# A 3x3 convolution on one core: output channels dealt to even and odd partitions, stored by halves

## The chip, the cores and the metric

The kernel runs on one core of a Trainium2 chip. The metric is the device time of the whole program in microseconds (us). The kernel before has a median of 126.94 us over 8 runs, from 126.81 to 127.33 us. The profile comes from one profiled execution with a time of 126.81 us; its trace spans 125.0 us, so 1.81 us of that time lie around the span.

## The reference

```python
batch, c_in, h, w, c_out = 16, 64, 64, 64, 128
x_pad = np.pad(x, ((0, 0), (0, 0), (1, 1), (1, 1)))
for b, co, ci, kh, kw:
    output[b, co] += weight[co, ci, kh, kw] * x_pad[b, ci, kh:kh+h, kw:kw+w]
```

(The five loops are drawn into one line here.) Input and output are float32. The input is 16 images of 64 channels, 64 x 64 pixels (16.8 MB); the output is 16 images of 128 channels, 64 x 64 pixels (33.6 MB). One channel of one image is 16,384 bytes, contiguous in memory, and a whole output image is 2 MB.

## The kernel before

The 16 images are worked on in 8 pairs, p = 0 to 7. The 64 channels of the first image of a pair stand in partitions 0 to 63, those of the second in partitions 64 to 127. The convolution is computed row pair by row pair with sums of two input rows (`sums`, tile `ss`), so that each block of 8 row pairs needs three groups of matmuls (`group`): one over `ss`, one for the even output rows and one for the odd ones. ScalarE copies the first group out of PSUM (tile `ut`, L188). VectorE adds it to the second group (L194) and to the third (L197) and writes the output tile `ot` in SBUF. `ot` has 128 partitions, one for each output channel, and per partition two images of 64 rows of 64 float32 values. Four such blocks make a pair.

**Weights.** The weights arrive as `w_raw`, one output channel per partition. VectorE casts them to float16 (`w16`, L88). Eighteen matmuls at L116 transpose them: the stationary operand is a slice of `w16`, the moving operand the 128 x 128 identity `ident`, which GpSimd makes. The column in which an output channel comes out in `wp` and then in `Wt` is the partition of `ot` in which it is computed; with `ident` channel c is in partition c.

**Input.** `load` (L63) brings a pair as one transfer of 2 MB, the first pair in four cuts. ScalarE casts it to float16 (tile `xs`, L75), and two pieces are cast by GpSimd. The first seven pairs are asked for at the start; the last, LATE = 7, when the store of pair 2 has been issued.

**Output.** When the last block of a pair is done, the pair is stored. All transfers, loads and stores, go through one queue, SyncE's (SP), in program order (`keep`). A store waits in that queue for the VectorE addition before it. Pairs 0 to 4 and 6 go out in one transfer each (L210: 128 partitions, two images of 16 KB each per partition). Pair 7 goes in two, after 32 and after 64 rows. Pair 5 is cut differently: its first image in one transfer (L205), the first 58 rows of its second image in another (L206), and the last 6 rows in two more (L208), of 124 and of 4 partitions. Four slots of 32 KB per partition hold first the input and then the output tiles: `ot` of pair p is in slot (p + 3) % 4.

**Transfers and semaphores.** In the built program the transfers take eight completion semaphores in rotation, and a transfer waits for the one that used its semaphore before it, eight transfers earlier. Loads and stores count alike.

Of the kernel before, what the change touches and what calls it, by code (L numbers as in the profile page):

```python
# [9 lines left out]
F16 = mybir.dt.float16  # L10
# [3 lines left out]
def kernel(  # L14
# [6 lines left out]
    nc = tc.nc  # L21
    B, CI, H, W = x.shape
    CO = weight.shape[0]
# [3 lines left out]

    keep = tc.keep_in_program_order
    x_rows = x.rearrange("b c h w -> (b c) h w")
    out_pairs = out.rearrange("(g b) co h w -> g co b h w", b=2)  # L30
    w_flat = weight.rearrange("co ci kh kw -> co (ci kh kw)")

    const = ctx.enter_context(tc.tile_pool(name="const", bufs=1))
# [20 lines left out]
    def load(p):  # L54
        if p >= 6:
            xf[p] = big.tile([128, H, W], F32, tag="single", name="xf")
        else:
            if p % 2 == 0:
                two[p // 2] = pair_slot(p // 2, [128, 2, H, W], "xf")
            xf[p] = two[p // 2][:, p % 2, :, :]  # L60
        for lo, hi in cuts if p == 0 else [(0, H)]:
            keep(
                nc.sync.dma_start(  # L63
                    xf[p][:, lo:hi, :], x_rows[128 * p : 128 * p + 128, lo:hi, :]
                )
            )
# [3 lines left out]
    def cast(p, n):  # L70
        if p not in xs:
            xs[p] = xpool.tile([128, H, W], F16, tag=f"xs{p % 4}", name="xs")
        lo, hi = cuts[n]
        copy = nc.gpsimd.tensor_copy if (p, n) in by_pool else nc.scalar.copy
        keep(copy(xs[p][:, lo:hi, :], xf[p][:, lo:hi, :]))  # L75
# [3 lines left out]
    def outs(p):  # L79
        ots[p] = pair_slot((p + 3) % 4, [128, 2, H // 2, 2, W], "ot")  # L80
# [3 lines left out]
    outs(0)  # L84
    ident = const.tile([128, 128], F16)
    make_identity(nc, ident)
    w16 = const.tile([CO, CI * 9], F16)
    keep(nc.vector.tensor_copy(w16, w_raw))  # L88

# [3 lines left out]
    def sums(eng, p, src, lo, n):  # L93
        if p not in ss:
            ss[p] = spool.tile([128, H // 2, W], F16, tag="ss", name="ss")
        v = src.rearrange("p (j i) c -> p j i c", i=2)
        keep(
            eng.tensor_add(  # L98
                ss[p][:, lo : lo + n, :], v[:, lo : lo + n, 0, :], v[:, lo : lo + n, 1, :]
            )  # L100
        )
# [9 lines left out]
    for kh in (1, 2, 0):  # L111
        wp = psum.tile([128, 512], F32, tag="acc", name="wp")
        for k in range(3):
            t = 3 * kh + k
            for q in (0, 64):
                nc.tensor.matmul(wp[q : q + 64, k * CO : k * CO + CO], w16[:, t::9], ident)  # L116
        wps[kh] = wp[:, 0 : 3 * CO]
    keep(nc.scalar.copy(wrow(G1), wps[1]))  # L118
    sums(nc.vector, 0, xf[0], 0, RB)
# [16 lines left out]
    for p in range(NP):  # L136
        if p not in ots:
            outs(p)
        if p + 1 < NP:
            for lo in (0, 16):  # L140
                sums(nc.gpsimd, p + 1, xf[p + 1] if p in (0, 1, 6) else xs[p + 1], lo, 16)
            if p == 1 or p == 2:
                cast(2 * p + 1, 3)
        for blk in range(4):
            j0 = blk * RB

            def group(wi_rows):

                tiles = [
                    psum.tile([128, RB, W], F32, tag="acc", name="acc") for _ in range(2)  # L150
                ]
                n = 3 * len(wi_rows)
                i = 0
                for wi, off in wi_rows:
                    for kw in (1, 0, 2):
                        c_lo, c_hi = max(0, 1 - kw), min(W, W + 1 - kw)
                        for b2 in range(2):
                            p0 = 64 * b2
                            lo, hi = j0, j0 + RB
                            if off is None:  # L160
                                rhs = ss[p][p0 : p0 + 64, lo:hi, c_lo + kw - 1 : c_hi + kw - 1]
                            else:
                                while 2 * lo + off < 0:
                                    lo += 1
                                while 2 * (hi - 1) + off > H - 1:
                                    hi -= 1
                                first = 2 * lo + off
                                last = 2 * (hi - 1) + off
                                rhs = xs[p][
                                    p0 : p0 + 64,  # L170
                                    first : last + 1 : 2,
                                    c_lo + kw - 1 : c_hi + kw - 1,
                                ]
                            nc.tensor.matmul(  # L174
                                tiles[b2][:, lo - j0 : hi - j0, c_lo:c_hi],
                                Wt[p0 : p0 + 64, wi, kw, :],
                                rhs,
                                start=i == 0,
                                stop=i == n - 1,
                            )  # L180
                        i += 1
                return tiles

            U = group([(G1, None)])
            us = []
            for b2 in range(2):
                ut = upool.tile([128, RB, W], F32, tag="ut", name="ut")
                keep(nc.scalar.copy(ut, U[b2]))  # L188
                us.append(ut)
            for q, n in casts[p][blk]:  # L190
                cast(q, n)
            A = group([(G21, 1), (G0, -1)])
            for b2 in range(2):
                nc.vector.tensor_add(ots[p][:, b2, j0 : j0 + RB, 0, :], A[b2], us[b2])  # L194
            Bt = group([(G01, 0), (G2, 2)])
            for b2 in range(2):
                nc.vector.tensor_add(ots[p][:, b2, j0 : j0 + RB, 1, :], Bt[b2], us[b2])  # L197
            parts = {3: (0, 64)} if p < NP - 1 else {1: (0, 32), 3: (32, 64)}
            if blk in parts:
                lo, hi = parts[blk]  # L200
                src = ots[p].rearrange("p b j i c -> p b (j i) c")
                dst = out_pairs[p]
                if p == 5:

                    keep(nc.sync.dma_start(dst[:, 0, :, :], src[:, 0, :, :]))  # L205
                    keep(nc.sync.dma_start(dst[:, 1, 0:58, :], src[:, 1, 0:58, :]))  # L206
                    for q0, q1 in ((0, 124), (124, 128)):
                        keep(nc.sync.dma_start(dst[q0:q1, 1, 58:64, :], src[q0:q1, 1, 58:64, :]))  # L208
                else:
                    keep(nc.sync.dma_start(dst[:, :, lo:hi, :], src[:, :, lo:hi, :]))  # L210
                if p == 2:
                    load(LATE)
# [28 lines left out]
```

## Time and profile before

| what | value |
|---|---|
| median of 8 runs, lowest, highest | 126.94, 126.81, 127.33 us |
| profiled execution: own time, span | 126.81, 125.0 us |
| TensorE busy, share of the span | 105.5 us, 84% |
| VectorE busy | 84.2 us, 67% |
| ScalarE busy | 65.5 us, 52% |
| GpSimd busy | 33.4 us, 27% |
| last VectorE addition, start and length of the last two | 110.99 us, 1.28 us |
| issue of the last store | 112.30 us |
| bytes read from and written to HBM | 17.07 MB, 33.55 MB |
| DMA packets | 4338, 50.77 MB |

The profile counts an engine as busy while one of its instructions runs. The DMA engines, 16 for the core, have a row of their own with their mean busy share, and one with the rate. Two views name what the end of the program hangs on: the chain of work that ended last, which is followed back from the last instruction, and the table of stretches, which gives for any stretch of time the busy time of each engine and the busy share of the DMA engines. The records under these views hold each DMA packet with its start, its length and its size, but not the DMA engine that moved it. A packet of 4 bytes is a completion mark: each DMA engine that takes part in a transfer writes one when its part is done.

### The profile page before, as it was taken

To read this page: it belongs to the slowest core of one execution; us is meant where nothing else is said; L and a number is where in the kernel's file an instruction comes from. 1 tells how busy PE (TensorE), PEld (TensorE's weight loads), DVE (VectorE), ACT (ScalarE), POOL (GpSimd) and SP (SyncE) were. 2 spreads that over 40 slices of the span, in tenths; PEclk is the share of its full clock that TensorE was granted. 3 is DMA by queue.
4 is the path that set the end of the run, shared out by engine and by line. 5 is a ranking of instruction groups with operands and counts; after the bars stand their busy time and mean duration, and the time that the engine had idled before them with its cause. 6 is when DMAs were issued, how large, how long until landed. Compare 5 with 4: busy or idle time off the path is not lost.

```text
span 125.0 us, 2428 instructions
## 1 busy us (share of the span) xinstructions
PE 105.5 (84%) x978; PEld 53.3 (43%) x978; DVE 84.2 (67%) x135; ACT 65.5 (52%) x98; POOL 33.4 (27%) x22
## 2 busy tenths in 40 slices
PE   0489999999999999999999999999999999940000
PEld 0334545545555455455554555445454554510000
DVE  0288777777777777777877787778777788870000
ACT  4283899999789886666333333334666533300000
POOL 2000396930870075006700570049000000000000
PEclk9999999999999999999999999999999999999555
DMA  4999999999999999999999999999999999999981
GB/s 115 314 437 440 430 425 419 430 446 425 425 430 422 419 438 435 430 430 419 414 425 446 430 419 440 430 419 419 435 435 421 429 407 432 427 417 419 427 375 50
DMA packets 4338, 50.77 MB, mean 406 GB/s; under 512 B 360, under 2 KB 488, under 8 KB 1128
## 3 DMA queue, kind: packets, MB, share of 16 engines
q1 hardware_dynamic: 4328, 50.63, 96.4%
q8 instruction: 7, 0.11, 0.3%
q14 instruction: 3, 0.02, 0.0%
HBM read 17.07 MB, written 33.55 MB: 405 GB/s over the span
## 4 chain that ended last, share of the span: by engine, by line
PE 82%; DMA 4%; DVE 2%; issue 1%; DVEq 0%; SPq 0%
PE acc L174 82%; DMA xf<-in_x_dram 4%; DVE ot L194 1%; DVE ss L98 1%; DVE ot L197 0%; DVEq L236 0%; SPq L48 0%; DVEq L194 0%
## 5 line engine op out<-in xcount | busy, mean ns | idle before, releaser
L174 PE MATMUL acc<-xs,Wt 64*128 64x504 f16 (+3 forms) x768 | 88.3, 376 | 0.0
L174 PEld LDWEIGHTS <-Wt 64*128 64x128 f16 x960 | 52.2, 95 | 52.9 <-issue 2.8
L194 DVE TENSOR_TENSOR ot<-acc,ut 128x512 f32<-128x512 f32 x64 | 41.2, 686 | 21.6 <-PE acc L174 18.0
L188 ACT COPY ut<-acc 128x512 f32<-128x512 f32 x64 | 34.4, 590 | 39.3 <-issue 35.2
L197 DVE TENSOR_TENSOR ot<-acc,ut 128x512 f32<-128x512 f32 x64 | 41.1, 684 | 0.0
L75 ACT CAST xs<-xf 128x1024 f16<-128x1024 f32 (+2 forms) x30 | 30.9, 1065 | 0.6 <-DMA xf<-in_x_dram 0.6
L174 PE MATMUL acc<-ss,Wt 64*128 64x504 f16 (+1 forms) x192 | 27.0, 384 | 1.1 <-DVE ss L98 1.1
L98 POOL TENSOR_TENSOR ss<-xs 128x1024 f16<-128x1024 f16 x8 | 16.8, 2127 | 30.4 <-PE acc L174 30.4
L98 POOL TENSOR_TENSOR ss<-xf 128x1024 f16<-128x1024 f32 x6 | 14.1, 2369 | 23.2 <-DMA xf<-in_x_dram 14.6
L116 PE MATMUL wp<-ident,w 128*64 128x128 f16 x18 | 1.3, 328 | 4.3 <-DVE w L88 4.3
L98 DVE TENSOR_TENSOR ss<-xf 128x512 f16<-128x512 f32 x4 | 2.8, 689 | 2.6 <-DMA xf<-in_x_dram 2.6
L88 DVE CAST w<-w_raw 128x576 f16<-128x576 f32 x1 | 0.5, 460 | 3.7 <-DMA w_raw<-in_weight_dram 3.7
L116 PEld LDWEIGHTS <-w 128*64 128x64 f16 x18 | 1.1, 210 | 4.3 <-DVE w L88 4.3
L118 ACT CAST Wt<-wp 128x384 f16<-128x384 f32 x1 | 0.5, 480 | 2.9 <-PE wp L116 2.9
L75 POOL CAST xs<-xf 128x896 f16<-128x896 f32 x2 | 1.9, 934 | 0.0
L118 ACT ACT_TABLE_LOAD x1 | 1.3, 1283 | 0.7 <-PEq L225 0.7
L123 ACT CAST Wt<-wp 128x384 f16<-128x384 f32 x1 | 0.5, 479 | 0.5 <-DVE Wt L121 0.5
L120 DVE TENSOR_TENSOR Wt<-wp,Wt 128x384 f16<-128x384 f32 x1 | 0.6, 551 | 0.0
L121 DVE TENSOR_TENSOR Wt<-wp,Wt 128x384 f16<-128x384 f32 x1 | 0.5, 548 | 0.0
L124 ACT CAST Wt<-wp 128x384 f16<-128x384 f32 x1 | 0.5, 484 | 0.0
masks.py:199 POOL TENSOR_SCALAR_AFFINE_SELECT ident<-ident 128x128 f16<-128x128 f16 x1 | 0.3, 292 | 0.1
masks.py:197 POOL MEMSET ident<- 128x128 f16 x1 | 0.2, 204 | 0.3 <-POOLq L225 0.3
(4 smaller groups left out, 0.4 us busy)
## 6 DMA issues: line engine op xcount, KB each, us to landing
out_dram<-ot SPq DMA_DIRECT2D x6, 4096.0 KB, 20.8
xf<-in_x_dram SPq DMA_DIRECT2D x7, 2048.0 KB, 21.0
out_dram<-ot SPq DMA_DIRECT2D x3, 2048.0 KB, 13.5
out_dram<-ot SPq DMA_DIRECT2D x1, 1856.0 KB, 17.7
xf<-in_x_dram SPq DMA_DIRECT2D x2, 512.0 KB, 5.7
xf<-in_x_dram SPq DMA_DIRECT2D x1, 576.0 KB, 4.8
xf<-in_x_dram SPq DMA_DIRECT2D x1, 448.0 KB
w_raw<-in_weight_dram SPq DMA_DIRECT2D x1, 288.0 KB, 3.0
```

Of the source, the lines that this page charges most:

```text
L75: keep(copy(xs[p][:, lo:hi, :], xf[p][:, lo:hi, :]))
L88: keep(nc.vector.tensor_copy(w16, w_raw))
L98: eng.tensor_add(ss[p][:, lo : lo + n, :], v[:, lo : lo + n, 0, :], v[:, lo : lo + n, 1, :])
L116: nc.tensor.matmul(wp[q : q + 64, k * CO : k * CO + CO], w16[:, t::9], ident)
L118: keep(nc.scalar.copy(wrow(G1), wps[1]))
L120: keep(nc.vector.tensor_sub(wrow(G21), wps[2], wrow(G1)))
L121: keep(nc.vector.tensor_sub(wrow(G01), wps[0], wrow(G1)))
L123: keep(nc.scalar.copy(wrow(G0), wps[0]))
L174: nc.tensor.matmul(tiles[b2][:, lo - j0 : hi - j0, c_lo:c_hi], Wt[p0 : p0 + 64, wi, kw, :], rhs, start=i == 0, stop=i == n - 1,)
L188: keep(nc.scalar.copy(ut, U[b2]))
L194: nc.vector.tensor_add(ots[p][:, b2, j0 : j0 + RB, 0, :], A[b2], us[b2])
L197: nc.vector.tensor_add(ots[p][:, b2, j0 : j0 + RB, 1, :], Bt[b2], us[b2])
```

## The change

The weights are transposed with another matrix, `spread`, in place of `ident`. `spread` is a copy of `ident` with its columns reordered, so that output channel e * 64 + q (e = 0 or 1, q = 0 to 63) comes out in partition 2q + e. Channels 0 to 63 are thus in the even partitions of `ot`, channels 64 to 127 in the odd ones. Each store becomes two: e = 0 stores the even partitions, which is 64 channels that lie side by side in memory, and e = 1 the odd ones. Of pair 5, the even half goes out in one transfer; the odd half is cut into its first image, the first 56 rows of its second image, and the last 8 rows of that image in three transfers of 57, 3 and 4 partitions.

```diff
-    out_pairs = out.rearrange("(g b) co h w -> g co b h w", b=2)
+    out_pairs = out.rearrange("(g b) (e q) h w -> g e q b h w", b=2, e=2)
...
     make_identity(nc, ident)
+
+    spread = const.tile([128, 128], F16)
+    nc.vector.tensor_copy(
+        spread.rearrange("p (q e) -> p e q", e=2), ident.rearrange("p (e q) -> p e q", e=2)
+    )
     w16 = const.tile([CO, CI * 9], F16)
...
-                nc.tensor.matmul(wp[q : q + 64, k * CO : k * CO + CO], w16[:, t::9], ident)
+                nc.tensor.matmul(wp[q : q + 64, k * CO : k * CO + CO], w16[:, t::9], spread)
...
-                dst = out_pairs[p]
-                if p == 5:
-
-                    keep(nc.sync.dma_start(dst[:, 0, :, :], src[:, 0, :, :]))
-                    keep(nc.sync.dma_start(dst[:, 1, 0:58, :], src[:, 1, 0:58, :]))
-                    for q0, q1 in ((0, 124), (124, 128)):
-                        keep(nc.sync.dma_start(dst[q0:q1, 1, 58:64, :], src[q0:q1, 1, 58:64, :]))
-                else:
-                    keep(nc.sync.dma_start(dst[:, :, lo:hi, :], src[:, :, lo:hi, :]))
+                for e in range(2):
+                    dst = out_pairs[p, e]
+                    if p == 5 and e == 1:
+
+
+                        keep(nc.sync.dma_start(dst[:, 0, :, :], src[1::2, 0, :, :]))
+                        keep(nc.sync.dma_start(dst[:, 1, 0:56, :], src[1::2, 1, 0:56, :]))
+                        for q0, q1 in ((0, 57), (57, 60), (60, 64)):
+                            keep(nc.sync.dma_start(
+                                dst[q0:q1, 1, 56:64, :],
+                                src[2 * q0 + 1 : 2 * q1 : 2, 1, 56:64, :],
+                            ))
+                    else:
+                        keep(nc.sync.dma_start(
+                            dst[:, :, lo:hi, :], src[e::2, :, lo:hi, :]
+                        ))
```

## The prediction

> **What bounds the kernel now.** I read the page's slices first, then the queue table, then the chain that ended last.
>
> ```profile
> span 125.0 us, 2428 instructions
> ...
> PE   0489999999999999999999999999999999940000
> ...
> DMA  4999999999999999999999999999999999999981
> GB/s 115 314 437 440 430 425 419 430 446 425 425 430 422 419 438 435 430 430 419 414 425 446 430 419 440 430 419 419 435 435 421 429 407 432 427 417 419 427 375 50
> ...
> q1 hardware_dynamic: 4328, 50.63, 96.4%
> ...
> PE 82%; DMA 4%; DVE 2%; issue 1%; DVEq 0%; SPq 0%
> ```
>
> The chain says TensorE, but it is followed back from the last compute instruction, which ends at 112.3 us; TensorE has zeros in the last four slices. The DMA row is full from the second slice to the 38th, at 407 to 446 GB/s after the first two. The queue's packets fill 96.4% of 16 engines' 125.0 us, that is 120.5 us for each engine. So the 16 DMA engines bound the program, and the question is when the last of them runs dry. The table by stretches shows that end (columns: stretch and length, busy time and instructions of PE, PEld, DVE, ACT, POOL, granted clock, DMA share, GB/s):
>
> ```profile
> 10.00:38.00 28.00, 28.00 (x266) 14.14 (x264) 22.33 (x37) 23.34 (x33) 15.41 (x8) 1.00 1.01 430
> 41.00:67.00 26.00, 26.00 (x247) 13.09 (x245) 20.43 (x34) 15.51 (x24) 8.42 (x4) 1.00 1.01 428
> ...
> 120.00:120.60 0.60, 0.00 (x0) 0.00 (x0) 0.00 (x0) 0.00 (x0) 0.00 (x0) 0.50 1.03 437
> 120.60:121.40 0.80, 0.00 (x0) 0.00 (x0) 0.00 (x0) 0.00 (x0) 0.00 (x0) 0.50 0.78 328
> 121.40:122.30 0.90, 0.00 (x0) 0.00 (x0) 0.00 (x0) 0.00 (x0) 0.00 (x0) 0.50 0.48 200
> 122.30:122.90 0.60, 0.00 (x0) 0.00 (x0) 0.00 (x0) 0.00 (x0) 0.00 (x0) 0.50 0.23 96
> 122.90:123.20 0.30, 0.00 (x0) 0.00 (x0) 0.00 (x0) 0.00 (x0) 0.00 (x0) 0.50 0.13 55
> 123.20:123.80 0.60, 0.00 (x0) 0.00 (x0) 0.00 (x0) 0.00 (x0) 0.00 (x0) 0.50 0.07 27
> ```
>
> Loads (first row) and stores (second) both keep the engines full. From 120.6 us they run dry one after another. Length by share from there is 0.62 + 0.43 + 0.14 + 0.04 + 0.04 = 1.27 us; spread evenly, the work would end near 121.9 us, against 123.7. So no rebalancing can gain more than about 1.9 us, and only the latest engine counts.
>
> The packet records name no engine, but packets follow one another without gaps, so each engine's chain can be followed. The last store's 16 completion marks stand at 120.64 to 120.81 (four engines), 121.54 to 122.24 (eight), 122.84, 123.13, 123.68 and 123.73 us. Two things make the late ones. (a) The 128 packets of 1536 bytes of L208 form four chains of 32, 61.3 ns apart, 1.97 us each, the first from 100.76, the last to 103.61 us. Followed on, these four engines end at 122.24, 122.84, 123.68 and 123.13; the third also met an instruction packet of 8192 bytes at 107.16 (about 0.65 us). (b) One other engine, with no such packets, has nearly all its 16 KB store packets at 634 to 653 ns where others have 611, from about 40 to 111 us; its loads and the 8 KB packets of pair 7 are normal. About 110 packets by 36 ns are 3.9 us. It ends last, at 123.73.
>
> **The change, part by part.** Engines per transfer: 128 partitions gave 16 marks, 124 gave four chains of 31, 4 gave four of one: the largest divisor up to 16 each time. By this 64 gives 16 engines, 57 and 3 three each, 4 four. The two transfers of L208 used the same four engines, so I take the three to be among those four; no row shows it.
>
> Separate rows. Before, 128 x 1536 = 196,608 bytes on four engines; after, 64 x 2048 = 131,072 bytes, 19 + 1 + 1 = 21 packets on three engines and one on the fourth. The other 65,536 bytes go to all 16: 4096 bytes each, 0.15 us at 611 ns per 16 KB. A 2048-byte packet I put at 81 ns, between 61.3 ns (1536) and 140 ns (3584): 21 make 1.70 us. Three of the four so change by -1.97 + 1.70 + 0.15 = -0.12 us, the fourth by -1.97 + 0.08 + 0.15 = -1.74, the other twelve by +0.15, the last one among them.
>
> More transfers. Full-width stores go from 10 to 19: nine more completion marks per engine. The mark is 9 ns, the next packet starts 6 ns after it: 0.07 us on all.
>
> SP's queue:
>
> ```profile
> L210 SPq DMA_DIRECT2D out_dram<-ot x8: 372/382/405, 22.6 to 112.3; - x8
> L208 SPq DMA_DIRECT2D out_dram<-ot x2: 799/801/803, 87.9 to 88.7; - x2
> L205 SPq DMA_DIRECT2D out_dram<-ot x1: 344/344/344, 86.1 to 86.1; - x1
> L206 SPq DMA_DIRECT2D out_dram<-ot x1: 1133/1133/1133, 86.7 to 86.7; - x1
> ...
> DMA to landing us min/median/max: 11.9/16.3/23.1
> ```
>
> A second half is issued some 0.4 us after the first and is needed 4.9 us later (8 packets by 611 ns): hidden by the first half. Pair 5 takes 0.38 + 0.34 + 1.13 + 3 x 0.80 = 4.3 us of SP from 86.1, and pair 6 is not ready before 99.49. The late load of pair 7 waits for ScalarE's cast, not for SP. If this cover were gone, a pair would pay the 0.4 us. With eight semaphores and twice the stores, a transfer waits for one eight earlier, now four pairs' worth: the tightest is the 4-partition transfer at about 90 us, behind pair 3's second half, which lands at 84.2. No wait binds; nothing is queued behind one.
>
> The copy to `spread`:
>
> ```profile
> 1.01 0.29 POOL masks.py:199 TENSOR_SCALAR_AFFINE_SELECT ident<-ident 128x128 f16<-128x128 f16 x1
> 3.75 0.46 DVE L88 CAST w<-w_raw 128x576 f16<-128x576 f32 x1 [3.75 <-DMA w_raw<-in_weight_dram]
> ```
>
> It is 128 x 128, so at most the 0.46 us of L88, and starts at 1.30; VectorE waits for the weights until 3.75. Hidden by 2 us; uncovered it would delay the first matmul by up to 0.46. TensorE's work and its shapes stay.
>
> Half-width transfers: their rate is in no row. Both bounds come from near rows. For a loss: while the four chains of L208 walked through partitions that other engines' packets also came from, the small ones kept 61.3 ns, and 16 KB packets beside them took up to 642 ns; the excess sums to about 0.11 us in 8 us of such walking, 1.4%. If each engine shares partitions' ways with another for all 78 us of stores, that is 1.1 us. For a gain: (b)'s 36 ns may belong to the partitions or addresses which that engine serves, and a new dealing may end it; it is then no longer last. I take neither: 78 us at the old rate, (b) as before.
>
> A rule speaks against the change: the Trainium skill, "DMA: Bandwidth & Descriptors", Rules for kernel authors, calls two transfers to disjoint partition halves not worth it and asks for one of 128 partitions, and the page gives about 2.0 us fixed per transfer. Nine more by that, each exposed, would be an estimated +18 us; the row of share 1.01 above shows transfers queued back to back, so it does not enter the sum.
>
> Sum for the last engine: 123.73 + 0.15 + 0.07 = 123.95, so +0.22 us. Against the profiled time 126.81 that is 127.03, against the median of 126.94 it is 127.16. I say 127.1.
>
> **The rivals.** Under 0.2% (0.25 us) a measurement of this kernel can hardly tell from no change: 126.69 to 127.19 is "same".
>
> Rival 1, faster: the slow engine (b) gets other rows and keeps 611 ns. For it: slowness in stores alone, on one engine alone, looks like something of its rows. Against: the 8 KB packets to the same channels were normal, so it may belong to that engine while compute runs. The end passes to the four. If the fourth, relieved of 1.74 us, is the one at 123.68, then 123.13 - 0.05 = 123.08 is last: -0.65 us, 126.3. If not, 123.68 - 0.05 = 123.63: -0.10, 126.8.
>
> Rival 2, slower: each half makes two engines draw on the same partition group all through the stores. Price 1.1 us on top of 0.22: 128.3. For it: the 642 ns packets. Against: the small packets lost nothing. It decides as soon as a 16 KB store packet takes over 613 ns in the mean beyond (b): 128 packets by 2 ns are the 0.25 us.
>
> Rival 3, the halves do not use all 16 engines at once: if eight at a time, 78 us of stores become 156, about 205 us. Against: 4 and 124 partitions took as many engines as their divisors allow, and 64 allows 16.
>
> **How the numbers follow.** Forecast 0.36, own range 126.9 to 127.4: same 0.24, slower 0.12. Rival 1 0.36: faster 0.31, same 0.05. Rival 2 0.26 and rival 3 0.02: slower. Faster 0.31, same 0.29, slower 0.40. The range goes from 126.2, rival 1 with 0.1 to spare, to 128.3, rival 2 in full; beyond lie rival 3 and a larger contention.
>
> **What would show it.** Right: DMA share 1.0 and about 428 GB/s in the stores, one engine with 16 KB packets near 645 ns, its mark last, near 124 us; three chains of 21 packets of 2048 bytes, about 81 ns apart; the copy over before 3.75 us. Wrong: all packets at 611 ns and an end near 123.1 (rival 1); a store rate under 425 GB/s with packets longer on many engines (rival 2); a store waiting on SP for a landing, or L88 starting later, would break the parts costed at nothing.

## The result and the profile after

The changed kernel has a median of 127.57 us over 24 runs, the kernel before 127.14 us over 64 runs on the same chips. The ratio is 1.004, with a 95% interval from 1.003 to 1.005: +0.51 us, from 0.38 to 0.64; the two medians differ by 0.43 us. Ratios, here and below, are taken over the runs in the faster of two states of the chip, and a difference given as +x us is that of the ratio. The profiled execution took 127.55 us, with a span of 125.8 us.

The page's slices of the change, DMA busy share and rate:

```profile
span 125.8 us, 2442 instructions
...
DMA  4999999999999999999999999999999999999970
GB/s 130 287 410 445 427 433 417 438 427 433 422 433 430 433 420 433 422 438 422 412 448 427 422 422 438 422 443 417 433 427 427 420 412 437 433 406 427 425 336 16
DMA packets 4420, 50.77 MB, mean 404 GB/s; under 512 B 506, under 2 KB 506, under 8 KB 1210
```

The same bytes go out at the same rate; only the end is longer. There are 146 more packets under 512 bytes, the completion marks of the further transfers. The table by stretches (stretch and length, five engines, clock, DMA share, GB/s), in most of the stretches shown of before and one more:

```profile
41.00:67.00 26.00, 26.00 (x248) 13.44 (x244) 20.43 (x34) 15.65 (x24) 8.42 (x4) 1.00 1.01 428
...
120.60:121.40 0.80, 0.00 (x0) 0.00 (x0) 0.00 (x0) 0.00 (x0) 0.00 (x0) 0.50 0.85 358
121.40:122.30 0.90, 0.00 (x0) 0.00 (x0) 0.00 (x0) 0.00 (x0) 0.00 (x0) 0.50 0.67 282
122.30:122.90 0.60, 0.00 (x0) 0.00 (x0) 0.00 (x0) 0.00 (x0) 0.00 (x0) 0.50 0.17 68
122.90:123.20 0.30, 0.00 (x0) 0.00 (x0) 0.00 (x0) 0.00 (x0) 0.00 (x0) 0.50 0.13 55
123.20:123.80 0.60, 0.00 (x0) 0.00 (x0) 0.00 (x0) 0.00 (x0) 0.00 (x0) 0.50 0.07 27
123.80:124.40 0.60, 0.00 (x0) 0.00 (x0) 0.00 (x0) 0.00 (x0) 0.00 (x0) 0.50 0.03 14
```

The stores run at 428 GB/s as before, so half-width stores of dealt channels cost no rate. At the end a share of 0.06 is one engine of sixteen. From 123.2 us at most one works, and by the marks it is alone from 123.21 to 124.29 us. It is the slow engine of the prediction: nearly all its 16 KB store packets again take 634 to 662 ns, from 40 to 111 us.

The copy to `spread` and the cast that follows it, from the timeline of the change:

```profile
1.34 0.24 DVE L89 COPY spread<-ident 128x128 f16<-128x128 f16 x1 [1.34 <-POOL ident masks.py:199]
3.67 0.46 DVE L93 CAST w<-w_raw 128x576 f16<-128x576 f32 x1 [2.09 <-DMA w_raw<-in_weight_dram]
```

The copy is done at 1.58 us and VectorE then waits 2.09 us for the weights. It is hidden.

One profile stands for one execution, and this matters here. The kernel before, profiled a second time (e12 below), had a span of 125.4 us and took 127.25 us. So the 0.8 us between the first two spans are not the change's cost. What repeats is read between two marks of the slow engine in the same profile, from the end of pair 0's store on. Its marks in us, from the packet records:

| kernel | end of pair 0 | end of pair 4 | end of pair 5 | last | pair 0 to last |
|---|---|---|---|---|---|
| before | 47.93 | 93.96 | 103.79 | 123.73 | 75.80 |
| before, second profile (e12) | 48.39 | 94.40 | 104.24 | 124.18 | 75.79 |
| the change | 48.13 | 94.29 | 104.32 | 124.29 | 76.16 |
| e1, rows alone | 48.44 | 94.47 | 104.50 | 124.39 | 75.95 |
| e2, by image | 47.98 | 94.12 | 103.96 | 123.94 | 75.96 |
| e7, halves without separate rows | 48.13 | 94.27 | 104.59 | 124.55 | 76.43 |

The start scatters by 0.5 us, also between two executions of one kernel; the last column agrees within 0.01 us in the two profiles of before. By it the slow engine loses 0.36 us in the change: 0.13 in pairs 1 to 4, 0.20 in pair 5, 0.04 in pairs 6 and 7. The first two are clear of scatter: pairs 1 to 4 take 46.01 to 46.04 us in the profiles that store them at full width (before, e12, e1, e5, e8 and e9) and 46.13 to 46.15 in those that store them in two equal parts with 16 KB packets (the change, e2, e7 and e11). The 0.04 is not: with pairs 6 and 7 stored as before, e1 has 19.89 us for them and e5 19.99, against 19.94. The rest of the 0.51 us lies after the last packet.

### The profile page after: what moved, and what is told of

Read it like the earlier page. It is cut to its first block, busy times and chain, and to the rows that moved or that the text cites. A ratio compares the mean times of both kernels' runs of the same rounds, so it can differ in the third digit from the quotient of the medians.

```text
span 125.8 us, 2442 instructions
## 1 busy us (share of the span) xinstructions
PE 105.9 (84%) x978; PEld 54.6 (43%) x978; DVE 84.6 (67%) x136; ACT 65.5 (52%) x98; POOL 33.4 (27%) x22
## 4 chain that ended last, share of the span: by engine, by line
PE 82%; DMA 4%; DVE 2%; issue 1%; DVEq 0%; SPq 0%
PE acc L179 82%; DMA xf<-in_x_dram 4%; DVE ot L199 1%; DVE ss L103 1%; DVE ot L202 0%; DVEq L248 0%; SPq L48 0%; DVEq L199 0%
## 5 line engine op out<-in xcount | busy, mean ns | idle before, releaser
L179 PEld LDWEIGHTS <-Wt 64*128 64x128 f16 x960 | 53.5, 95 | 52.2 <-issue 3.4
L121 PE MATMUL wp<-spread,w 128*64 128x128 f16 x18 | 1.3, 327 | 4.2 <-DVE w L93 4.2
```

The source lines that it names most:

```text
L179: nc.tensor.matmul(tiles[b2][:, lo - j0 : hi - j0, c_lo:c_hi], Wt[p0 : p0 + 64, wi, kw, :], rhs, start=i == 0, stop=i == n - 1,)
```

## The experiments

Each was timed against the kernel before on the same chip, in five rounds unless said. The edits are cuts from the diffs, with broken lines joined.

**e1, the separate rows alone.**

```diff
-   keep(nc.sync.dma_start(dst[:, 1, 0:58, :], src[:, 1, 0:58, :]))
-   for q0, q1 in ((0, 124), (124, 128)):
-       keep(nc.sync.dma_start(dst[q0:q1, 1, 58:64, :], src[q0:q1, 1, 58:64, :]))
+   keep(nc.sync.dma_start(dst[:, 1, 0:56, :], src[:, 1, 0:56, :]))
+   for q0, q1 in ((0, 64), (64, 121), (121, 124), (124, 128)):
+       keep(nc.sync.dma_start(dst[q0:q1, 1, 56:64, :], src[q0:q1, 1, 56:64, :]))
```

> Full-width stores as before; only the separate rows of pair 5 are as in the change (the last 8 rows of channels 64 to 127 in 57, 3 and 4 partitions, 131,072 bytes; the same rows of channels 0 to 63 in one transfer of 64 partitions). Theory A (the engine that ends last gets 4096 bytes more, and nine more completion marks): only the bytes apply here, +0.15 us, and two marks, +0.01: +0.16 us, a ratio of 1.001. Rival B (the cost lies in the number of transfers or in half-width transfers): no more than +0.05 us. Rival C (the slow engine is slow because of what it stores): does not tell here.

Measured: 127.50 us against 127.03, ratio 1.0029 (1.0005 to 1.0053), +0.37 us with a wide interval. The slow engine's pair 5 took 10.03 us in place of 9.84, +0.20 as in the change; pairs 1 to 4 took 46.02 as before, and pairs 6 and 7 0.05 less. Theory A's mechanism holds. But the last landing was followed by 0.99 us, where the profile of before has 0.83: a term that theory A does not have.

**e2, more transfers at full width.**

```diff
-   keep(nc.sync.dma_start(dst[:, :, lo:hi, :], src[:, :, lo:hi, :]))
+   for b2 in range(2):
+       keep(nc.sync.dma_start(dst[:, b2, lo:hi, :], src[:, b2, lo:hi, :]))
```

> Channels not dealt, all 128 partitions in every store, but each store of the other pairs cut in two by image: eight more transfers, packets still 16 KB, separate rows as before. Theory A with marks at 7 ns each: +0.06 us. Rival B1 (each further transfer costs more than its mark, in the engines or at the end of the program): +0.25 to +0.4 us, a ratio of 1.002 to 1.003. Rival B2 (half-width transfers are what costs): +0.06 us, as theory A.

Measured: 127.22 us against 127.03, ratio 1.0013 (0.9998 to 1.0029). The interval takes in both zero and B1's lower end and settles nothing by itself. The marks do: from pair 0 to pair 4 the slow engine takes 46.14 us, as in the change (46.15) and against 46.02 before. Four more transfers cost it 0.11 to 0.14 us, 28 to 35 ns each, whether they are halves of the partitions or of the images. Half width is not what costs; on this engine a transfer costs more than the 7 ns of its mark. On the other engines it does not: between two marks they take 9.719 us for 16 packets of 611 ns before, and 4.862 for 8 in the change and in e2, so that a further transfer costs them 5 ns.

**e3, halves of neighbouring partitions.**

```diff
-   keep(nc.sync.dma_start(dst[:, :, lo:hi, :], src[:, :, lo:hi, :]))
+   for q0 in (0, 64):
+       keep(nc.sync.dma_start(dst[q0 : q0 + 64, :, lo:hi, :], src[q0 : q0 + 64, :, lo:hi, :]))
```

> Channels not dealt; the stores of all pairs but pair 5 in halves of 64 neighbouring partitions, 0 to 63 and 64 to 127. Theory A: the halves run on all 16 engines at the old rate, +0.06 us. Rival B2 (engines that draw on the same group of partitions disturb each other): here 16 engines share 64 neighbouring partitions, so it should be worse than dealt halves, +1 us or more. If the halves reach only half of the ways into SBUF at a time, stores go at some 215 GB/s and the time rises by up to 68 us (seven of eight pairs, 78 us of stores doubled).

Measured: 175.07 to 181.81 us in six runs, against 127.03. The ratio of 1.385 (1.377 to 1.393), +49 us, rests on the two shortest, 175.07 and 177.18; the profile is of a run of 181.74. Its stretches, same columns as above; the first holds loads, the next two mostly stores, the last pair 5's two full-width transfers among them:

```profile
10.00:27.00 17.00, 17.00 (x162) 8.81 (x160) 13.54 (x23) 14.41 (x20) 10.33 (x5) 1.00 1.01 430
...
57.00:84.00 27.00, 27.00 (x256) 13.96 (x254) 21.10 (x34) 10.35 (x19) 8.43 (x4) 1.00 1.00 260
90.00:140.00 50.00, 26.09 (x198) 11.82 (x194) 19.78 (x32) 11.20 (x18) 4.66 (x2) 0.76 1.00 302
```

The DMA share stays at 1.00 while the rate falls to 260 GB/s, and to 242 from 42 to 57 us, where only half stores run. All 16 engines are busy, but a 16 KB packet takes 1.3 us in the median from 40 to 60 us, and single ones up to 2.7 us later. From 140 us on the engines also end far apart, the last at 178.7. A full DMA row does not say that the DMA engines move at their rate; the GB/s beside it does. The dealing of channels is thus what makes half-width stores harmless. The even or the odd partitions give full rate, the lower or the upper 64 do not.

**e4, packets of 8 KB.** Each store is cut in two by rows, pair 5's two large transfers as well.

```diff
-   keep(nc.sync.dma_start(dst[:, :, lo:hi, :], src[:, :, lo:hi, :]))
+   for r0 in range(lo, hi, 32):
+       keep(nc.sync.dma_start(dst[:, :, r0 : r0 + 32, :], src[:, :, r0 : r0 + 32, :]))
```

> Channels not dealt, full width, each store cut in two by rows, so that all store packets have at most 8192 bytes; eight more transfers by pairs and two more in pair 5. If the slow engine (16 KB store packets at 644 where others have 611 ns) is slow per large packet, its 3.9 us vanish and it ends near 120 us; the end passes to the engine at 123.68: -0.05 us and some 0.07 for marks, so no change (within 0.1 us), with a final mark of another engine. If it is slow as long as compute runs, its 8 KB packets take some 322 ns before 111 us and it still ends last: +0.07 us.

Measured: 127.48 us against 127.03, ratio 1.0036 (1.0021 to 1.0051). The slow engine's 8 KB store packets took 15 ns more than 309 in the median until 112 us, and nothing more in pair 7's stores after that; it ended last, at 124.36. It is slow by time, not by packet size. The +0.46 us are above the +0.07 expected, and they lie between the marks: from pair 0 to the last the slow engine takes 76.25 us, 0.45 more than before, 0.27 of it in pairs 1 to 4. The cut doubles the store packets there besides adding transfers, and what each of the two costs was not measured apart.

**e5, two small transfers more.** The separate rows of before in two times three rows.

```diff
-   for q0, q1 in ((0, 124), (124, 128)):
-       keep(nc.sync.dma_start(dst[q0:q1, 1, 58:64, :], src[q0:q1, 1, 58:64, :]))
+   for r0 in (58, 61):
+       for q0, q1 in ((0, 124), (124, 128)):
+           keep(nc.sync.dma_start(dst[q0:q1, 1, r0 : r0 + 3, :], src[q0:q1, 1, r0 : r0 + 3, :]))
```

> The kernel before, with the separate rows of pair 5 in two times three rows: two more transfers, on the four engines of the separate rows alone, same bytes per engine. The last store then uses the second of the eight completion semaphores, as in the change, instead of the eighth; SP checks the eighth last. Theory A' (the change costs 0.20 us for bytes, about 0.15 for marks, and about 0.17 because the last landing is followed by further checks on SP): the time from the last landing to the end of the span goes from 0.83 to 1.00 us, and the kernel is +0.17 us slower, ratio 1.0013. Rival (the 1.00 us are chance): 0.83 us, no change.

Measured: from the last landing (124.54 us) to the end of the span (125.53) 0.99 us, as theory A' says. The time was 127.56 us against 127.21, ratio 1.0034 (1.0016 to 1.0052): more than the 1.0013 expected, and just above it at the lower end. The slow engine's stages account for some 0.08 us more, the rest is open.

**e6, separate rows on fifteen engines.**

```diff
-   for q0, q1 in ((0, 124), (124, 128)):
+   for q0, q1 in ((0, 120), (120, 128)):
```

> The kernel before, with the 6 separate rows of pair 5 in transfers of 120 and 8 partitions instead of 124 and 4. By largest divisors they run on 15 and 8 engines: eight packets of 1536 bytes on fifteen engines, a ninth on eight of them, none on one. If the slow engine is the one left out: it ends as before, near 123.73, and all others get some 0.5 us, the four of before lose 1.5 us: the time stays within 0.05 us of before (it is last alone). If it is one of the fifteen, its chain shows 8 or 9 packets of 1536 bytes and it ends 0.49 or 0.55 us later, near 124.25: +0.5 us, ratio 1.004.

Measured: 127.86 us against 127.21, ratio 1.0053 (1.0035 to 1.0071), +0.67 us. The slow engine's chain shows nine packets of 1536 bytes, eight and one, and it ended last at 124.79, alone from 123.01 on. So it takes part in a transfer on eight engines and in none on four.

**e7, the change without separate rows.**

```diff
-   if p == 5 and e == 1:
+   if False:
```

> The change with pair 5 stored like the others, in two plain halves without separate rows. All 16 engines get 8192 bytes more in the even part than in the change, 0.31 us, three small transfers and one mark fewer, -0.03 us, and the last store moves to the sixth semaphore (0.05 to 0.15 us less at the end). Theory A': the slow engine ends 0.28 us later than in the change, the kernel is +0.65 us to +0.75 us against before, ratio 1.005 to 1.006. Rival (the separate transfers of 57, 3 and 4 are what costs): equal to before or better.

Measured: 128.12 us against 127.21, ratio 1.0067 (1.0049 to 1.0086), +0.85 us, with +0.65 to +0.75 expected and inside the interval. The slow engine's pair 5 takes 10.32 us, 0.48 more than before and 0.28 more than in the change. The transfers of 57, 3 and 4 are not what costs; they earn about 0.3 us. The rival falls.

**e8 and e9, separate rows on seven engines.** Ten rows (e8) or fourteen (e9) of pair 5, half of them from each image; the rest of the pair goes in one transfer.

```diff
-   keep(nc.sync.dma_start(dst[:, 0, :, :], src[:, 0, :, :]))
-   keep(nc.sync.dma_start(dst[:, 1, 0:58, :], src[:, 1, 0:58, :]))
-   for q0, q1 in ((0, 124), (124, 128)):
-       keep(nc.sync.dma_start(dst[q0:q1, 1, 58:64, :], src[q0:q1, 1, 58:64, :]))
+   keep(nc.sync.dma_start(dst[:, :, 0:59, :], src[:, :, 0:59, :]))
+   for q0, q1 in ((0, 119), (119, 126), (126, 128)):
+       keep(nc.sync.dma_start(dst[q0:q1, :, 59:64, :], src[q0:q1, :, 59:64, :]))
```

> The kernel before, with ten separate rows in pair 5 (five of each image) in transfers of 119, 7 and 2 partitions, which by largest divisors run on engines 0 to 6 (17 + 1 partitions each) and two of them. The slow engine took part in the transfer on eight engines of e6 and in none on four of before, so it is one of the numbers 4 to 7. If it is 7: it has none of the separate rows and 4 rows less in the even part, 0.31 us less than before, and ends 0.3 us earlier, unless one of 4 to 6, which gain 1.6 us, is then last: between -0.3 us and no change, ratio 0.998 to 1.000. If it is 4, 5 or 6, its chain shows the separate packets (36 of 1280 bytes, about 1.9 us) and the kernel is 1.6 us slower, ratio 1.012.

> As e8 with fourteen rows (seven of each image). If the slow engine is 7, it ends 0.61 us earlier than before, but the seven others carry 36 packets of 1792 bytes, about 2.5 us, so one of them can be last: between -0.5 us and +0.4 us. Otherwise 2.2 us slower.

Measured: e8 128.50 us against 127.07, ratio 1.0107 (1.0088 to 1.0125); e9 129.04, ratio 1.0143 (1.0119 to 1.0168), +1.8 us where 2.2 were expected. The edit shown is that of e8. In both, the slow engine's chain runs through the small packets, and it ends alone, at 125.40 and 126.09, the next at 123.93 and 123.69. It is one of the seven. An attempt to relieve it by a transfer that leaves it out would have to stay on fewer engines, as before already does. No version tried beats the kernel before.

**e10, no compute** (one execution). The kernel keeps the loads and full-width stores and leaves out all casts, sums, matmuls and additions.

```diff
+   zero = pair_slot(3, [128, 2, H, W], "ot")
+   keep(nc.vector.memset(zero, 0.0))
...
+           keep(nc.sync.dma_start(out_pairs[p][:, :, lo:hi, :], zero[:, :, lo:hi, :]))
```

> All loads and stores of the kernel before in the same sizes and order on SP, but no cast, sum, matmul or addition: one VectorE memset fills a tile, and all stores read that tile, so the output is zero. The separate rows are left out too. If the slow engine is slow because compute runs: all 16 KB store packets take 611 ns and none 630 to 660, and the last marks have no outlier. If it is slow whatever runs: one engine still has about 110 store packets near 644 ns.

Measured: a span of 123.5 us. Its stretches (columns: stretch and length, DVE, POOL, clock, DMA share, GB/s):

```profile
41.00:67.00 26.00, 0.00 (x0) 0.00 (x0) 1.00 1.01 431
76.00:98.00 22.00, 0.00 (x0) 0.00 (x0) 1.00 1.01 433
```

From 75 to 115 us every 16 KB packet takes 611 ns in the mean of each 5 us, and none is longer than 640; other packets over 640 are only where the late load and the stores meet, from 65 to 75 us, one at 36.7 us, and among the first loads near 9 us. The last 16 marks stand between 120.84 and 122.17, 1.3 us apart where before has 3.1; the separate rows left out are part of that. With compute gone, no engine is slow. All stores here read one tile, in slot 3, but that alone is not the reason: in the kernel before pair 4 is stored from slot 3 too, and the slow engine's packets there took 634 to 653 ns. What of compute does it (operands in SBUF, instruction supply, the records of the profile itself) was not tried.

**e11, the change with its last store on the eighth semaphore.** Two transfers fewer:

```diff
-   for lo, hi in cuts if p == 0 else [(0, H)]:
+   for lo, hi in cuts[:2] + [(34, H)] if p == 0 else [(0, H)]:
...
-   keep(nc.sync.dma_start(dst[:, 0, :, :], src[1::2, 0, :, :]))
-   keep(nc.sync.dma_start(dst[:, 1, 0:56, :], src[1::2, 1, 0:56, :]))
+   keep(nc.sync.dma_start(dst[:, :, 0:60, :], src[1::2, :, 0:60, :]))
    for q0, q1 in ((0, 57), (57, 60), (60, 64)):
        keep(nc.sync.dma_start(
-           dst[q0:q1, 1, 56:64, :], src[2 * q0 + 1 : 2 * q1 : 2, 1, 56:64, :],
+           dst[q0:q1, :, 60:64, :], src[2 * q0 + 1 : 2 * q1 : 2, :, 60:64, :],
        ))
```

> The changed kernel with two transfers fewer, so that its last store uses the eighth completion semaphore, as in the kernel before: the separate rows are four of each image in place of eight of one (same bytes, 57, 3 and 4 partitions), the odd half of pair 5 otherwise one transfer, and the first pair's third and fourth cut are loaded as one. Theory A': from the last landing to the end of the span 0.83 us in place of 1.00, two marks fewer on the slow engine (-0.05): -0.2 us against the change, ratio to before near 1.0025. Rival (the end has nothing to do with the semaphore's number): 1.00 us and a ratio of 1.0035 to 1.004.

Measured: 127.33 us against 127.00, ratio 1.0023 (1.0012 to 1.0034), and 0.83 us from the last landing (125.03) to the end of the span (125.86). SP's waits for the stores at the end, from the waits of SP (engine and line, what was waited for; us in total, times, longest), first in the kernel before:

```profile
SPq L236 <- DMA out_dram<-ot: 11.3, 3, 4.8
```

The same view of the change:

```profile
SPq L248 <- DMA out_dram<-ot: 9.8, 1, 9.8
```

And of e11:

```profile
SPq L247 <- DMA out_dram<-ot: 9.4, 4, 2.4
```

The records of SP's last instructions show the order: it asks for two semaphores at a time, 3 and 2, 4 and 1, 5 and 0 (counted from zero), then for 6, then for 7. In the change the last store has number 1, so SP sits in one long wait and still has three more waits to walk through once that store has landed, at 124.82, 124.88 and 124.94 us, some 0.06 us each. In before and e11 it has number 7, which is asked last, and the others were walked through while stores were still running. In e7 it has number 5, two waits are left, and the end takes 0.95 us. So 0.17 to 0.18 us of the change hang on this.

**e12, the kernel before once more** (one execution), the unchanged file.

> The kernel before, profiled a second time. In four of the profiles so far whose program up to pair 5 is that of before, the slow engine ended the store of pair 0 at 48.21 to 48.44 us, against 47.93 in the profile of before. If that is scatter between executions, this profile has it at 47.9 to 48.5, with the last landing followed by 0.83 us.

Measured: pair 0's end at 48.39 us, last landing 124.62, span 125.45: 0.83 us. The profile of before was an early one of its kind.

## Why the prediction was right, and where it was not

The range of 126.2 to 128.3 us held the 127.57. The forecast of a change too small to tell did not: +0.22 us was forecast, +0.51 (0.38 to 0.64) measured, over the 0.25 us that I called the same. The forecast's own range, 126.9 to 127.4, missed it as well: 127.57 lies in the whole range only because that goes up to the full price of rival 2, which did not come, and that is luck. The kernel before took 127.14 here, 0.20 more than the 126.94 the forecast started from. The mechanism was right; one term of the sum was too small and one was missing.

- **What bounds the kernel**: right. The latest DMA engine sets the end, and it is the engine named under (b), 0.05 us later than the next before (0.42 in e12) and 1.08 after.
- **Separate rows**, +0.15 us on the last engine: right. Pair 5 takes 0.20 us more, of which one further transfer makes 0.03 to 0.04; the rest is 4096 bytes at that engine's 644 ns per 16 KB, 0.16 us. The chains came as worked out: 21 packets of 2048 bytes on three engines, 80 ns apart (81 was put), and one on a fourth.
- **More transfers**, 9 x 7 ns = 0.07 us: the mechanism right, the size wrong for the engine that counts. Pairs 1 to 4 show 0.13 us for four transfers, 33 ns each, and pairs 6 and 7 0.04 us for three, which is within that stage's scatter. With pair 5's that is 0.20 us for eight; pair 0's could not be read because of the scatter. I priced the mark and the gap after it, which holds for the other engines (5 ns). The slow engine pays more while compute runs; in pair 7, after compute, it too pays only 5 to 14 ns a transfer (the change, e2, e7 and e11). Why was not shown. e2 shows the same price at full width. The 2.0 us per transfer that the prediction left out of the sum show in no run.
- **The end**, not in the sum: 0.18 us. I had looked at the semaphores for waits before a transfer and not for the order in which the last ones are asked. e5 and e11 show it in both directions. Together 0.16 + 0.20 + 0.18 = 0.54 us, within the measured interval.
- **Half-width transfers at the old rate**: right, 428 GB/s, for dealt partitions. The bound of 1.1 us taken from packets that crossed other engines' partitions was harmless for these, and far too small for neighbouring halves, which cost some 49 us in e3.
- **(b) as before**: right, rival 1 falls. The slowness follows neither rows nor addresses (dealing changes both), nor packet size (e4); it goes with compute (e10), by one execution, and what of compute makes it is open.
- **Rival 2**: no mean rise of packets, it falls. From 76 to 96 us the 16 KB store packets of the other engines take 611.8 ns in the mean before and after. **Rival 3** falls for the change, and e3 shows how near it lies.
- **Parts costed at nothing**: the copy was hidden with 2.09 us to spare, and no store waited for another store's landing. One waited 0.9 us for a load's, in the kernel before as well. SP's issues were underpriced. From the view of the tile `ot` of the change (line, count; shortest, median and longest issue in ns, first and last start):

```profile
L220 SPq DMA_DIRECT2D out_dram<-ot x17: 600/652/1405, 23.2 to 113.5; - x17
L215 SPq DMA_DIRECT2D out_dram<-ot x3: 802/812/896, 89.8 to 91.6; - x3
...
DMA to landing us min/median/max: 9.5/15.2/26.1
```

A half-width issue takes 600 ns and more where a full one took 372 to 405. It stayed hidden behind 9.5 us and more of queue.

## What to carry to other kernels

Where the DMA engines are full, follow each one to its last packet: a transfer that relieves four engines and adds 4 KB to the one that ends last makes the kernel slower. Price a further transfer by what it costs the latest engine, here about 30 ns where the others pay 5, and look at which semaphore the last transfer gets. If a store has to be split by partitions, take every second one and not neighbouring halves, and read the GB/s beside the busy share.

## What the runs showed of the hardware

- Sixteen DMA engines moved 242 GB/s where they only stored 64 neighbouring partitions at a time (e3, 42 to 57 us); every second of 128 partitions gave 428. The Trainium skill, "SBUF — State Buffer", section "Door 1: The DMA port swizzle (why `[64,N]` ≈ `[32,N]`)", says that partitions 0 to 63 reach 8 of 16 ports and puts that at some 218 GB/s; e3 agrees in kind and lies above the figure. Its map also gives the even partitions all 16 ports, which the change's 428 GB/s fit.
- The same page, section "Who interferes with whom", says that DMA never contends with a compute engine. On one DMA engine store packets took 644 ns in place of 611 while compute ran, and 611 without it (e10). Whether that is contention in SBUF was not shown, but a plan cannot take the 5% for zero.
- The number of engines of a transfer was the largest divisor up to 16 of its partitions in every case that could be counted: 124 gave four, 57 three, 120 and 8 gave the slow engine eight packets and one (e6).
